# Encoder trunk on one Trainium2 core: the last expert's gate in two column halves, the last two blocks' norm steps shared, and a fixed order of ScalarE and VectorE at the end

## Chip, core and metric

The kernel runs on one core of a Trainium2 chip. The core has TensorE (PE; its weight loads are shown apart as PEld), VectorE (DVE), ScalarE (ACT), GpSimd (POOL) and SyncE (SP), and each works through its own queue in order. The metric is the device time of one execution in microseconds, less is better.

## The reference, cut to what matters

One layer of an encoder trunk over 512 tokens of 1024 numbers: a mixer, then 16 experts of which each takes the 64 tokens that like it best, then an embedding that is gated per token, and a last norm.

```python
def rmsnorm(x, g):
    y = xf * lax.rsqrt(jnp.mean(xf * xf, axis=-1, keepdims=True) + EPS)
    return (y * g.astype(jnp.float32)).astype(x.dtype)
...
        x = x + expert_choice_ffn(rmsnorm(x, norm2_g[i]), w_router[i], w_e_gate[i],
                                  w_e_up[i], w_e_down[i])
        gate = jax.nn.sigmoid(rmsnorm(x, norm3_g[i]) @ w_ple_gate[i])
        x = x + gate * (p[i] @ w_ple_proj[i])
    return rmsnorm(x, final_g)
```

The change lies in the last three lines. The sigmoid is made of a tanh: sigmoid(v) = 0.5 (1 + tanh(v / 2)).

## The kernel before, in words

The tokens stand in four blocks of 128 rows, `X[0]` to `X[3]`, each 128 x 1024. Experts 0 to 13 are added into the blocks in pairs. The rows of the last two experts, 14 and 15, go another way: the 64 tokens of each are gathered into a tile `xg[0]` or `xg[1]` of 128 x 512 (a token's 1024 columns lie in two partitions, 64 apart), the expert's output is added there, gate and last norm are done on that tile, and the rows are scattered into the output by GpSimd. So at the end two streams of work run beside each other: the four blocks, and the two tiles of rows.

For the blocks `base(i, k0, k1)` multiplies with the gate's weight (`w_ple_gate`, split into high and low parts by `gsplit`, three products for each): i = 0, 1 are the two column halves of blocks 0 and 1, i = 2, 3 those of blocks 2 and 3. Its sums stand in two PSUM tiles `zb[i][0]` and `zb[i][1]`, one for each block, and after the last product ScalarE copies them to SBUF, into `Z` (L1135; the profile names those tiles `w`). The loop at the end then does for each block b and half h: tanh (L1541, scaled with `r3`, half of the reciprocal root of the mean square), times the projected embedding plus one (L1542, VectorE), the addition to `X` (L1543, VectorE), and a square with a sum (`sumsq`, L983, ScalarE; its second record is the read of the accumulator). From the two sums of a block `rstd` makes the last norm's factor by three Newton steps, some ten short VectorE instructions that follow one another (L254 to L269), and VectorE multiplies the block by factor and weight at once (L1550). Blocks 0 and 1 are stored by SyncE, blocks 2 and 3 by GpSimd with an indirect DMA (`store`, L1521), since rows that the last experts took must be left out.

For the tiles of rows, `finish_start` transposes, `finish_gate` multiplies (`paired`, L1247: 16 products of 512 columns, with 64-wide weights, two records for each), `finish_gated` does tanh (L1412), times the embedding (L1413), addition (L1414) in two halves of 256 columns, sums of squares, and the product with the weight (L1416); `row_rstd` adds the sums across the partitions on TensorE (L1382) and makes the root, and `finish_end` scales (L1421). Row tile 14 is finished while `base(3, ...)` runs; `c15`, the gate of expert 15, is TensorE's last large product.

What sets the order: a scheduler places the instructions of each engine by the order in which the program is written, and by priority where data are ready; `later(n)` puts what is inside n places back. TensorE alone has an order by hand: `in_order` chains all of its instructions after `mark` as they are written.

Of the kernel before, what the change touches and what calls it, by code (L numbers as in the profile page):

```python
# [12 lines left out]
AF = mybir.ActivationFunctionType  # L13
ALU = mybir.AluOpType
# [35 lines left out]
TAIL = (4, 5, 6, 7) + (8,) + (9, 10, 11, 12, 13, 4, 5, 6) + (7, 9, 10, 11) + (12,)  # L50
SOON = 3
FAR = 4096.0
SM = {}


# [137 lines left out]
def in_order(tc, nc, mark, engine):  # L193

    last, on = None, False
    for i in list(nc.cur_bb.bb.instructions):
        if on and i.engine == engine:
            if last is not None:
                tc.add_manual_dep(i, last.name, mybir.DependencyInfo(
                    mybir.DependencyClass.NoSync, mybir.DependencyReason.DATA), reason="in order")  # L200
            last = i
        on = on or i is mark
# [7 lines left out]
def _body(ctx, tc, nc, A, out):  # L210
# [7 lines left out]
    def ps(tag):  # L218
        return psum.tile([128, 512], F32, name=f"ps_{tag}", tag=tag, bufs=NBANK[tag])
# [24 lines left out]
    def small(n, tag, dt=F32, bufs=8):  # L244
        return tiny.tile([128, 16], dt, name=tag, tag=tag, bufs=bufs)[:, :n]
# [331 lines left out]
    @contextmanager  # L577
    def later(n):
        c = tc.cur_priority
        tc.cur_priority = c + n  # L580
        yield
        if n:
            tc.cur_priority = c
# [398 lines left out]
    def sumsq(t, acc, junk):  # L982
        act.activation(junk, t, AF.Square, accum_out=acc)  # L983
# [136 lines left out]
    def base(i, k0, k1):  # L1120
        bp, h = divmod(i, 2)
        if k0 == 0:
            zb[i] = [ps("b"), ps("b")]
            if h == 0:
                z = place()
                Z.extend([z[:, 0:1024], z[:, 1024:2048]])
        for k in range(k0, k1):
            gh, gl = (ahead.pop(0) if ahead else gsplit(k, h))[:2]
            for j in range(2):
                hi, lo = xps[2 * bp + j, k // 4]  # L1130
                t = slice((k % 4) * 128, (k % 4 + 1) * 128)
                mm3(zb[i][j], hi[:, t], lo[:, t], gh, gl, k == 0, k == 7)
        if k1 == 8:
            for j in range(2):
                act.copy(Z[2 * bp + j][:, h * 512:(h + 1) * 512], zb[i][j])  # L1135

# [262 lines left out]
    def finish_factor(a):  # L1399

        r = row_rstd(a, "u")
        dve.tensor_scalar(r, r, 0.5, None, op0=ALU.mult)  # L1402
        return r

    def finish_gate(c, xgT, k0, k1):
        paired(c, xgT.rearrange("p (a b c) -> p a b c", a=4, b=2), [halves(w) for w in WG], k0, k1,
               (0, 4, 1, 5, 2, 6, 3, 7))

    def finish_gated(i, x_, c, r, zg, junk):

        for s in (slice(0, 256), slice(256, 512)):
            act.activation(zg[:, s], c[:, s], AF.Tanh, scale=r)  # L1412
            dve.scalar_tensor_tensor(zg[:, s], zg[:, s], 1.0, ppg[i][:, s], op0=ALU.add, op1=ALU.mult)  # L1413
            dve.tensor_add(x_[:, s], x_[:, s], zg[:, s])  # L1414
        a = row_sums(x_, "w", junk)
        dve.tensor_mul(x_, x_, fin)  # L1416
        return a

    def finish_end(x_, a):

        dve.tensor_scalar(x_, x_, row_rstd(a, "w"), None, op0=ALU.mult)  # L1421
# [81 lines left out]
    finish_gate(c14, xgT, 0, 8)  # L1503
    a15 = finish_start(xg[1], xgT2, zg2)
    a14 = finish_gated(0, xg[0], c14, r14, y14, xgT)
    base(3, 0, 4)
    r15 = finish_factor(a15)
    finish_end(xg[0], a14)
    base(3, 4, 8)
    c15 = ps("mm")  # L1510
    finish_gate(c15, xgT2, 0, 8)
    finish_end(xg[1], finish_gated(1, xg[1], c15, r15, zg2, xgT2))

    in_order(tc, nc, mark, pe.engine)


    stores = []

# [5 lines left out]
            tc.declare_no_dep(i.ins, j.ins, reason="the stores' rows are disjoint")  # L1524
        stores.append(i)

    s3 = small(8, "s3", bufs=1)
    for b in range(4):
        for h in range(2):
            s = slice(h * 512, (h + 1) * 512)  # L1530
            sumsq(X[b][:, s], s3[:, b * 2 + h:b * 2 + h + 1], nat)
    s3b = small(4, "s3b", bufs=1)
    dve.reduce_sum(s3b, s3.rearrange("p (b h) -> p b h", h=2), axis=AX.X)
    r3 = small(4, "r3", bufs=1)
    dve.tensor_scalar(r3, rstd(s3b, 1.0 / D), 0.5, None, op0=ALU.mult)
    for b in range(4):
        s4 = small(2, "s4", bufs=2)
        for h in range(2):
            s = slice(h * 512, (h + 1) * 512)
            z = Z[b][:, s]  # L1540
            act.activation(z, z, AF.Tanh, scale=r3[:, b:b + 1])  # L1541
            dve.scalar_tensor_tensor(z, z, 1.0, pp[b][h], op0=ALU.add, op1=ALU.mult)  # L1542
            dve.tensor_add(X[b][:, s], X[b][:, s], z)  # L1543
            sumsq(X[b][:, s], s4[:, h:h + 1], nat)
        s4b = small(1, "s4b", bufs=2)
        dve.tensor_add(s4b, s4[:, 0:1], s4[:, 1:2])
        r4 = rstd(s4b, 1.0 / D)
        for h in range(2):
            s = slice(h * 512, (h + 1) * 512)
            dve.scalar_tensor_tensor(X[b][:, s], X[b][:, s], r4, gfb[h], op0=ALU.mult, op1=ALU.mult)  # L1550
        if b < 2:
            sp.dma_start(rows(out, b), X[b])
        else:
            store(out, xi[b - 2], X[b], T - 1)
    for i in range(2):
        store(out.rearrange("t (h d) -> (t h) d", h=2), dsti[i], xg[i], 2 * T - 1)

# [20 lines left out]
```

## Time and profile before

| what | us |
|---|---|
| median of 3 runs | 1073.98 |
| lowest and highest | 1073.71, 1075.87 |
| the profiled execution, its own time | 1077.42 |
| its span, first to last instruction | 1075.6 |
| TensorE busy | 1004.6 (93%) |
| VectorE busy | 485.4 (45%) |
| ScalarE busy | 336.5 (31%) |
| GpSimd busy | 38.4 (4%) |

All times in rows are microseconds from the span's start, and all are of the profiled execution. The runs without the profiler are some 3 us shorter. A row of a timeline gives start, busy time, engine, line and operation, what it writes and reads, the shape, and in brackets how long the engine had been idle and who ended that.

### The profile page before, as it was taken

Reading aid. Unit: us, or ns where it says so; the run is one execution under the profiler, and the core shown is the slowest. Engines: PE = TensorE matmul, PEld = TensorE weight load, DVE = VectorE, ACT = ScalarE, POOL = GpSimd, SP = SyncE. Lnnn points to the kernel's source line nnn. Section 1 sums busy time; section 2 is a strip of 40 time slices with the busy share of each in tenths; the row PEclk is TensorE's granted clock in tenths of the full one; section 3 lists DMA queues with packets and bytes.
Section 4 is the critical chain, followed back from the end, with each engine's and each line's share of the span. In section 5 each row is a group of like instructions: output and inputs, shape, how many; then the busy total and the mean of one; then the engine's idle time right before and its main releaser. Section 6 shows DMA issues by size and latency. Waiting matters only on the chain.

```text
span 1075.6 us, 12115 instructions
## 1 busy us (share of the span) xinstructions
PE 1004.6 (93%) x4566; PEld 601.4 (56%) x4566; DVE 485.4 (45%) x1082; ACT 336.5 (31%) x624; POOL 38.4 (4%) x45
## 2 busy tenths in 40 slices
PE   8999999999999999999499999998887898999996
PEld 5777887787668788878333333443232333346453
DVE  6896786645765545635710110221020204044646
ACT  6343325426553323423111112011101012145443
POOL 0022011000000000000000000000000000000001
PEclk9999999999999999999789999999999899999998
DMA  9322121322122653463879989999999999999601
GB/s 313 125 79 79 40 71 65 102 80 83 54 79 78 202 178 99 157 237 103 313 299 406 424 339 425 424 425 425 425 426 424 424 424 428 422 410 425 260 1 50
DMA packets 55491, 264.15 MB, mean 246 GB/s; under 512 B 6715, under 2 KB 11579, under 8 KB 31880
## 3 DMA queue, kind: packets, MB, share of 16 engines
q1 hardware_dynamic: 51072, 252.14, 59.1%
q0 software_dynamic: 1904, 6.44, 1.5%
q10 hardware_dynamic: 2456, 4.79, 1.4%
q8 instruction: 36, 0.59, 0.2%
q14 instruction: 23, 0.19, 0.0%
HBM read 258.88 MB, written 4.72 MB: 245 GB/s over the span
## 4 chain that ended last, share of the span: by engine, by line
PE 71%; DMA 17%; DVE 7%; ACT 2%; issue 2%; POOL 0%; POOLq 0%; SPq 0%; DVEq 0%; ACTq 0%
PE ps_mm L1230 12%; DMA w<-in_w_gu_dram 11%; PE ps_y L1247 8%; PE ps_mm L414 8%; PE ps_mm L413 8%; PE ps_mm L412 7%; DMA w<-in_w_dn_dram 4%; PE ps_b L412 3%; PE ps_b L413 3%; PE ps_b L414 3%; PE ps_pj L412 2%; PE ps_pj L413 1%; PE ps_mm L995 1%; PE ps_pj L414 1%; PE ps_mm L993 1%
## 5 line engine op out<-in xcount | busy, mean ns | idle before, releaser
L1230 PE MATMUL ps_mm<-w,xt 128*64 128x512 f32 x992 | 222.5, 596 | 17.1 <-DMA w<-in_w_gu_dram 17.1
L1230 PEld LDWEIGHTS ps_mm<-w,xt 128*64 128x64 f32 x992 | 70.7, 137 | 165.8 <-issue 124.0
L412 PE MATMUL ps_mm<-hhi,whi 128*128 128x512 f32 x392 | 156.9, 400 | 0.6 <-ACT whi L327 0.6
L414 PE MATMUL ps_mm<-hhi,wlo 128*128 128x512 f32 x392 | 155.3, 397 | 0.7 <-DVE wlo L329 0.5
L413 PE MATMUL ps_mm<-hlo,whi 128*128 128x512 f32 x392 | 154.7, 395 | 0.2 <-DVE hlo L363 0.2
L1234 DVE TENSOR_TENSOR sg<-sg,ps_mm 128x512 f32<-128x512 f32 x16 | 11.0, 688 | 262.3 <-PE ps_mm L1230 262.3
L1247 PE MATMUL ps_y<-w,hd 128*64 128x512 f32 x480 | 109.0, 607 | 6.2 <-ACT hd L1255 6.2
L327 ACT CAST whi<-w 128x1024 fp32r<-128x1024 f32 x50 | 52.6, 1051 | 123.6 <-PE ps_mm L413 64.7
L412 PEld LDWEIGHTS ps_mm<-hhi,whi 128*128 128x128 f32 x392 | 74.2, 189 | 19.6 <-ACT whi L327 2.1
L414 PEld LDWEIGHTS ps_mm<-hhi,wlo 128*128 128x128 f32 x392 | 74.0, 189 | 18.7 <-issue 2.5
L413 PEld LDWEIGHTS ps_mm<-hlo,whi 128*128 128x128 f32 x392 | 74.1, 189 | 17.8 <-issue 2.5
L1247 PEld LDWEIGHTS ps_y<-w,hd 128*64 128x64 f32 x480 | 34.9, 139 | 70.5 <-issue 61.5
L1233 ACT ACTIVATE sg<-ps_mm 128x512 f32<-128x512 f32 x16 | 9.6, 597 | 181.6 <-PE ps_mm L1230 181.6
L329 DVE TENSOR_TENSOR wlo<-w,whi 128x1024 fp32r<-128x1024 f32 x49 | 60.1, 1229 | 6.4 <-ACT whi L327 6.2
L1265 ACT ACTIVATE ys<-ps_y,ia 64x512 f32<-64x512 f32 x28 | 19.1, 682 | 100.2 <-PE ps_y L1247 99.8
L625 DVE TENSOR_TENSOR sg<-ps_mm,rbs 128x512 f32<-128x512 f32 x32 | 22.1, 689 | 47.3 <-PE ps_mm L414 46.8
L1094 DVE TENSOR_TENSOR yh<-ys,yh 128x512 fp32r<-128x512 f32 x14 | 9.1, 689 | 70.6 <-ACT yh L1093 70.0
L1115 DVE SCALAR_TENSOR_TENSOR gl<-w,sm,gh 128x512 fp32r<-128x512 f32 x32 | 24.0, 751 | 21.8 <-ACT gh L1114 21.7
L1166 POOL DMA_INDIRECT xe<-h2d,iai x8 | 7.7, 964 | 681.6 <-DVE num L1086 373.4
L1114 ACT ACTIVATE gh<-w,sm 128x512 fp32r<-128x512 f32 x32 | 23.0, 723 | 28.0 <-PE ps_b L414 20.4
L626 ACT ACTIVATE sg<-sg,hbg 128x512 f32<-128x512 f32 x32 | 23.1, 721 | 12.8 <-DVE sg L625 12.8
L413 PE MATMUL ps_b<-gl,xTh 128*128 128x512 f32 x64 | 26.3, 410 | 0.2 <-DVE uo L1402 0.2
(505 smaller groups left out, 1522.5 us busy)
## 6 DMA issues: line engine op xcount, KB each, us to landing
w<-in_w_gu_dram SPq DMA_DIRECT2D x124, 1024.0 KB, 19.6
w<-in_w_dn_dram SPq DMA_DIRECT2D x60, 1024.0 KB, 19.6
w<-in_w_in_dram SPq DMA_DIRECT2D x50, 512.0 KB, 4.1
wb<-in_w_br_dram SPq DMA_DIRECT2D x32, 128.0 KB, 2.4
w<-in_w_out_dram SPq DMA_DIRECT2D x8, 512.0 KB, 4.1
we<-in_w_dn_dram SPq DMA_DIRECT2D x16, 256.0 KB, 8.4
we<-in_w_gu_dram SPq DMA_DIRECT2D x16, 256.0 KB, 6.1
w<-in_w_ple_gate_dram SPq DMA_DIRECT2D x4, 1024.0 KB, 21.1
```

The lines of the kernel that those rows point to most:

```text
L327: act.copy(hi, raw)
L329: (pool if key in PW else dve).tensor_sub(lo, raw, hi.bitcast(F32))
L412: pe.matmul(p, whi, mhi, start=start, stop=False)
L413: pe.matmul(p, whi, mlo, start=False, stop=False)
L414: pe.matmul(p, wlo, mhi, start=False, stop=stop)
L625: dve.tensor_mul(g, p, rbs)
L626: act.activation(g, g, AF.Tanh, bias=hbg[:, n * 8 + d:n * 8 + d + 1], scale=0.5)
L1114: i = act.activation(hi, v, AF.Copy, scale=S("g3", k))
L1115: dve.scalar_tensor_tensor(lo, v, S("g3", k), hi.bitcast(F32), op0=ALU.mult, op1=ALU.subtract)
L1230: pe.matmul(t[h * 64:(h + 1) * 64], x, w[k][h], start=k == 0, stop=k == 7)
L1247: pe.matmul(y[h * 64:(h + 1) * 64], lt[:, k % 4, k // 4, :], w[k][h], start=n == 0, stop=n == 7)
L1265: act.activation(ys[h][r], y[hs], AF.Copy, scale=ia[hs, 16 + e:17 + e])
```

## The change

The gate of expert 15 is written as two sets of products, for the columns 0 to 255 and 256 to 511 of the same PSUM tile `c15`. The first column halves of blocks 2 and 3 are carried further at once, up to the square and the product with the weight. For their second halves the copy out of PSUM goes: the tanh reads `zb[3]` itself. For blocks 2 and 3 the weight is multiplied before the root is known (`weighed`), both blocks' roots are made together in instructions of two columns, and the factor is applied last: one half of block 2 on VectorE, the other half and block 3 on ScalarE. What follows the gate is written in one order by hand, and `in_order` now holds ScalarE and VectorE to it from `mark2` on. The blocks' steps before that stand earlier in the text, inside `later(FL)`.

```diff
--- before.py
+++ after.py
@@ -50,6 +50,7 @@
 TAIL = (4, 5, 6, 7) + (8,) + (9, 10, 11, 12, 13, 4, 5, 6) + (7, 9, 10, 11) + (12,)
 SOON = 3
 FAR = 4096.0
+FL = 400
 SM = {}
 
 
@@ -1130,7 +1131,7 @@
                 hi, lo = xps[2 * bp + j, k // 4]
                 t = slice((k % 4) * 128, (k % 4 + 1) * 128)
                 mm3(zb[i][j], hi[:, t], lo[:, t], gh, gl, k == 0, k == 7)
-        if k1 == 8:
+        if k1 == 8 and i < 3:
             for j in range(2):
                 act.copy(Z[2 * bp + j][:, h * 512:(h + 1) * 512], zb[i][j])
 
@@ -1503,16 +1504,6 @@
     finish_gate(c14, xgT, 0, 8)
     a15 = finish_start(xg[1], xgT2, zg2)
     a14 = finish_gated(0, xg[0], c14, r14, y14, xgT)
-    base(3, 0, 4)
-    r15 = finish_factor(a15)
-    finish_end(xg[0], a14)
-    base(3, 4, 8)
-    c15 = ps("mm")
-    finish_gate(c15, xgT2, 0, 8)
-    finish_end(xg[1], finish_gated(1, xg[1], c15, r15, zg2, xgT2))
-
-    in_order(tc, nc, mark, pe.engine)
-
 
     stores = []
 
@@ -1524,34 +1515,98 @@
             tc.declare_no_dep(i.ins, j.ins, reason="the stores' rows are disjoint")
         stores.append(i)
 
-    s3 = small(8, "s3", bufs=1)
-    for b in range(4):
-        for h in range(2):
-            s = slice(h * 512, (h + 1) * 512)
-            sumsq(X[b][:, s], s3[:, b * 2 + h:b * 2 + h + 1], nat)
-    s3b = small(4, "s3b", bufs=1)
-    dve.reduce_sum(s3b, s3.rearrange("p (b h) -> p b h", h=2), axis=AX.X)
-    r3 = small(4, "r3", bufs=1)
-    dve.tensor_scalar(r3, rstd(s3b, 1.0 / D), 0.5, None, op0=ALU.mult)
-    for b in range(4):
-        s4 = small(2, "s4", bufs=2)
-        for h in range(2):
-            s = slice(h * 512, (h + 1) * 512)
-            z = Z[b][:, s]
-            act.activation(z, z, AF.Tanh, scale=r3[:, b:b + 1])
-            dve.scalar_tensor_tensor(z, z, 1.0, pp[b][h], op0=ALU.add, op1=ALU.mult)
-            dve.tensor_add(X[b][:, s], X[b][:, s], z)
-            sumsq(X[b][:, s], s4[:, h:h + 1], nat)
-        s4b = small(1, "s4b", bufs=2)
-        dve.tensor_add(s4b, s4[:, 0:1], s4[:, 1:2])
-        r4 = rstd(s4b, 1.0 / D)
-        for h in range(2):
-            s = slice(h * 512, (h + 1) * 512)
-            dve.scalar_tensor_tensor(X[b][:, s], X[b][:, s], r4, gfb[h], op0=ALU.mult, op1=ALU.mult)
-        if b < 2:
+    def embedded(b, h, g):
+
+        s = slice(h * 512, (h + 1) * 512)
+        z = Z[b][:, s]
+        act.activation(z, g, AF.Tanh, scale=r3[:, b:b + 1])
+        dve.scalar_tensor_tensor(z, z, 1.0, pp[b][h], op0=ALU.add, op1=ALU.mult)
+        dve.tensor_add(X[b][:, s], X[b][:, s], z)
+
+    def squares(b, h):
+        sumsq(X[b][:, h * 512:(h + 1) * 512], s4[:, b * 2 + h:b * 2 + h + 1], nat)
+
+    def weighed(b, h):
+        s = slice(h * 512, (h + 1) * 512)
+        dve.tensor_mul(Z[b][:, s], X[b][:, s], gfb[h])
+
+    s4 = small(8, "s4", bufs=1)
+    s4b = small(4, "s4b", bufs=1)
+    with later(FL):
+        s3 = small(8, "s3", bufs=1)
+        for b in range(4):
+            for h in range(2):
+                s = slice(h * 512, (h + 1) * 512)
+                sumsq(X[b][:, s], s3[:, b * 2 + h:b * 2 + h + 1], nat)
+        s3b = small(4, "s3b", bufs=1)
+        dve.reduce_sum(s3b, s3.rearrange("p (b h) -> p b h", h=2), axis=AX.X)
+        r3 = small(4, "r3", bufs=1)
+        dve.tensor_scalar(r3, rstd(s3b, 1.0 / D), 0.5, None, op0=ALU.mult)
+        for b in range(2):
+            for h in range(2):
+                embedded(b, h, Z[b][:, h * 512:(h + 1) * 512])
+                squares(b, h)
+            dve.tensor_add(s4b[:, b:b + 1], s4[:, 2 * b:2 * b + 1], s4[:, 2 * b + 1:2 * b + 2])
+            r4 = rstd(s4b[:, b:b + 1], 1.0 / D)
+            for h in range(2):
+                s = slice(h * 512, (h + 1) * 512)
+                dve.scalar_tensor_tensor(X[b][:, s], X[b][:, s], r4, gfb[h], op0=ALU.mult, op1=ALU.mult)
             sp.dma_start(rows(out, b), X[b])
-        else:
-            store(out, xi[b - 2], X[b], T - 1)
+        for b in range(2, 4):
+            embedded(b, 0, Z[b][:, 0:512])
+            squares(b, 0)
+            weighed(b, 0)
+    base(3, 0, 4)
+    r15 = finish_factor(a15)
+    finish_end(xg[0], a14)
+    base(3, 4, 8)
+
+    c15 = ps("mm")
+    halved = [slice(0, 256), slice(256, 512)]
+    WH = [halves(w) for w in WG]
+    xt15 = xgT2.rearrange("p (a b c) -> p a b c", a=4, b=2)
+    a15 = small(2, "wa", bufs=2)
+    mark2 = nc.cur_bb.bb.instructions[-1]
+
+    def gate15(s):
+        paired(c15[:, s], xt15, [[w[:, s] for w in ws] for ws in WH], order=(0, 4, 1, 5, 2, 6, 3, 7))
+
+    def tanh15(s):
+        act.activation(zg2[:, s], c15[:, s], AF.Tanh, scale=r15)
+
+    def add15(s):
+        dve.scalar_tensor_tensor(zg2[:, s], zg2[:, s], 1.0, ppg[1][:, s], op0=ALU.add, op1=ALU.mult)
+        dve.tensor_add(xg[1][:, s], xg[1][:, s], zg2[:, s])
+
+    gate15(halved[0])
+    gate15(halved[1])
+    embedded(2, 1, zb[3][0])
+    embedded(3, 1, zb[3][1])
+    squares(2, 1)
+    tanh15(halved[0])
+    weighed(2, 1)
+    squares(3, 1)
+    add15(halved[0])
+    sumsq(xg[1][:, halved[0]], a15[:, 0:1], xgT2[:, halved[0]])
+    dve.tensor_add(s4b[:, 2:4], s4[:, 4:8].rearrange("p (b h) -> p b h", h=2)[:, :, 0],
+                   s4[:, 4:8].rearrange("p (b h) -> p b h", h=2)[:, :, 1])
+    weighed(3, 1)
+    r4 = rstd(s4b[:, 2:4], 1.0 / D)
+    tanh15(halved[1])
+    dve.tensor_scalar(Z[2][:, 0:512], Z[2][:, 0:512], r4[:, 0:1], None, op0=ALU.mult)
+    act.activation(Z[2][:, 512:1024], Z[2][:, 512:1024], AF.Copy, scale=r4[:, 0:1])
+    add15(halved[1])
+    sumsq(xg[1][:, halved[1]], a15[:, 1:2], xgT2[:, halved[1]])
+    dve.tensor_mul(xg[1], xg[1], fin)
+    for h in range(2):
+        s = slice(h * 512, (h + 1) * 512)
+        act.activation(Z[3][:, s], Z[3][:, s], AF.Copy, scale=r4[:, 1:2])
+    finish_end(xg[1], a15)
+    in_order(tc, nc, mark, pe.engine)
+    for engine in (act.engine, dve.engine):
+        in_order(tc, nc, mark2, engine)
+    for b in range(2):
+        store(out, xi[b], Z[2 + b], T - 1)
     for i in range(2):
         store(out.rearrange("t (h d) -> (t h) d", h=2), dsti[i], xg[i], 2 * T - 1)
 
```

ScalarE at the end, before, from the copy of block 3's last sums on (`X_3267` and `X_3268` are blocks 2 and 3, `w_6904` their `Z`; what an instruction waits for is in brackets):

```order
L1135 COPY w_6904<-ps_b 128x512 [waits PE_49]
L1541 ACTIVATE w_6904<-w_6904,r_7196 128x512 [waits Activation_49]
L983 ACTIVATE nat,s_7270<-X_3267 128x512 [waits DVE_49]
L983 ACTIVATE nat,s_7300<-X_3268 128x512 [waits Activation_49]
L983 ACTIVATE nat,s_7300<-X_3268 128x512 [waits DVE_49,Activation_49]
L1412 ACTIVATE zg<-ps_mm,uo 128x256 [waits PE_49]
L1412 ACTIVATE zg<-ps_mm,uo 128x256
L983 ACTIVATE xgT,wa<-xg 128x256 [waits DVE_49] x2
```

And in the changed kernel (L1522 is the blocks' tanh, L1575 the gate's, L1597 and L1603 the scales):

```order
L1522 ACTIVATE w_6904<-ps_b,r_7049 128x512 [waits PE_49] x2
L984 ACTIVATE nat,s_7036<-X_3267 128x512 [waits DVE_49]
L1575 ACTIVATE zg<-ps_mm,uo 128x256 [waits PE_49]
L984 ACTIVATE nat,s_7036<-X_3268 128x512 [waits DVE_49,Activation_49]
L984 ACTIVATE xgT,wa<-xg 128x256 [waits DVE_49]
L1575 ACTIVATE zg<-ps_mm,uo 128x256
L1597 ACTIVATE w_6904<-w_6904,ro 128x512 [waits DVE_49]
L984 ACTIVATE xgT,wa<-xg 128x256 [waits DVE_49]
L1603 ACTIVATE w_6904<-w_6904,ro 128x512 x2
```

The square of block 3's second half stood ahead of the gate's first tanh and stands behind it now; the second tanh of the gate has no wait of its own in either.

VectorE at the end, before, from the end of block 3's root on:

```order
L269 SCALAR_TENSOR_TENSOR ro<-rt,ri 128x1 [waits DVE_49]
L1550 SCALAR_TENSOR_TENSOR X_3268<-X_3268,ro,gfb 128x512 [waits DVE_49]
L1413 SCALAR_TENSOR_TENSOR zg<-zg,ppg 128x256 [waits Activation_49] x2
L1414 TENSOR_TENSOR xg<-xg,zg 128x256 [waits DVE_49] x2
L1550 SCALAR_TENSOR_TENSOR X_3268<-X_3268,ro,gfb 128x512
L1416 TENSOR_TENSOR xg<-xg,fin 128x512 [waits Activation_49]
L254 TENSOR_SCALAR wv<-ps_t 128x1 [waits PE_49]
```

And in the changed kernel, first up to the start of the shared root (L1531 is `weighed`, L1578 and L1579 are `add15`, L1591 adds both blocks' sums):

```order
L1531 TENSOR_TENSOR w_6904<-X_3267,gfb 128x512
L1578 SCALAR_TENSOR_TENSOR zg<-zg,ppg 128x256 [waits Activation_49]
L1579 TENSOR_TENSOR xg<-xg,zg 128x256 [waits DVE_49]
L1591 TENSOR_TENSOR s4b<-s_7036 128x2 [waits Activation_49]
L1531 TENSOR_TENSOR w_6904<-X_3268,gfb 128x512
L255 TENSOR_SCALAR rv<-s4b 128x2 [waits DVE_49]
```

and then from its last step on:

```order
L270 SCALAR_TENSOR_TENSOR ro<-rt,ri 128x2 [waits DVE_49]
L1596 TENSOR_SCALAR w_6904<-w_6904,ro 128x512 [waits DVE_49]
L1578 SCALAR_TENSOR_TENSOR zg<-zg,ppg 128x256 [waits Activation_49]
L1579 TENSOR_TENSOR xg<-xg,zg 128x256 [waits DVE_49]
L1600 TENSOR_TENSOR xg<-xg,fin 128x512 [waits Activation_49]
L255 TENSOR_SCALAR wv<-ps_t 128x1 [waits PE_49]
```

Both halves of the gate's multiply and addition stood together, behind the two roots; now the first half stands ahead of the shared root (twelve instructions) and the second behind it.

## Rows read from the trace of the kernel before

**Rows 1.** The page, its fourth part: the chain that ended last, by engine.
```profile
PE 71%; DMA 17%; DVE 7%; ACT 2%; issue 2%; POOL 0%; POOLq 0%; SPq 0%; DVEq 0%; ACTq 0%
```

**Rows 2.** By stage: length; busy PE, PEld, DVE, ACT, POOL; granted clock, DMA share, GB/s.
```profile
1057.25:1064.35 7.10, 7.09 (x33) 2.21 (x32) 6.08 (x24) 4.09 (x9) 0.00 (x0) 1.00 0.08 32
...
1069.00:1075.60 6.60, 0.00 (x0) 0.00 (x0) 1.85 (x10) 0.00 (x0) 1.60 (x2) 0.51 0.26 104
```

**Rows 3.** Timeline of GpSimd, the last three stores.
```profile
1064.61 1.03 POOL L1521 DMA_INDIRECT out_dram<-X,numi  x1 [7.86 <-DVE ri L269]
1068.36 1.25 POOL L1521 DMA_INDIRECT out_dram<-X,numi  x1 [2.72 <-DVE X L1550]
1071.41 0.99 POOL L1521 DMA_INDIRECT out_dram<-xg,numi  x1 [1.80 <-DVE xg L1421]
```

**Rows 4.** Timeline of TensorE: the gate of expert 15, and the sums of squares.
```profile
1057.25 7.09 PE L1247 MATMUL ps_mm<-w,xgT 128*64 128x512 f32 x32
1067.68 0.78 PE L1382 MATMUL ps_t<-wa,one 128*128 128x1 f32 x4 [3.35 <-ACT xgT L983]
```

**Rows 5.** Timeline of ScalarE from 1044 us on.
```profile
1044.00 0.47 ACT L1412 ACTIVATE xe<-ps_pj,uo 128x256 f32<-128x256 f32 x1 [10.93 <-PE ps_pj L1247]
...
1056.65 0.59 ACT L1135 COPY w<-ps_b 128x512 f32<-128x512 f32 x1 [1.62 <-PE ps_b L414]
1057.27 0.72 ACT L1541 ACTIVATE w<-w,r 128x512 f32<-128x512 f32 x1
...
1060.99 0.63 ACT L983 ACTIVATE nat<-X 128x512 f32<-128x512 f32 x1
1061.53 0.19 ACT L983 ACTIVATION_READ_ACCUMULATOR nat<-X 128x1 f32 x1
1064.38 0.84 ACT L1412 ACTIVATE zg<-ps_mm,uo 128x256 f32<-128x256 f32 x2 [2.67 <-PE ps_mm L1247]
...
1067.54 0.40 ACT L983 ACTIVATE xgT<-xg 128x256 f32<-128x256 f32 x1
1067.84 0.19 ACT L983 ACTIVATION_READ_ACCUMULATOR xgT<-xg 128x1 f32 x1
```

**Rows 6.** Timeline of VectorE from 1056 us on.
```profile
1058.03 0.69 DVE L1542 SCALAR_TENSOR_TENSOR w<-w,grow 128x512 f32<-128x512 f32 x1 [2.21 <-ACT w L1541]
1058.76 0.69 DVE L1543 TENSOR_TENSOR X<-X,w 128x512 f32<-128x512 f32 x1
1059.36 0.69 DVE L1542 SCALAR_TENSOR_TENSOR w<-w,pp 128x512 f32<-128x512 f32 x1
1060.08 0.69 DVE L1543 TENSOR_TENSOR X<-X,w 128x512 f32<-128x512 f32 x1
...
1065.33 0.75 DVE L1550 SCALAR_TENSOR_TENSOR X<-X,ro,gfb 128x512 f32<-128x512 f32 x1
1066.00 0.75 DVE L1413 SCALAR_TENSOR_TENSOR zg<-zg,ppg 128x256 f32<-128x256 f32 x2
...
1068.67 0.15 DVE L254 TENSOR_SCALAR wv<-ps_t 128x1 f32<-128x1 f32 x1
...
1070.64 0.49 DVE L1421 TENSOR_SCALAR xg<-xg,wo 128x512 f32<-128x512 f32 x1
```

**Rows 7.** Timeline of VectorE, its idle time under TensorE's products near 1035 us.
```profile
1037.13 0.88 DVE L1501 SCALAR_TENSOR_TENSOR xg<-ps_y,ia,xg 128x256 f32<-128x256 f32 x2 [2.94 <-PE ps_y L1247]
```

**Rows 8.** Timeline of TensorE: short products with 64-wide weights.
```profile
171.26 0.44 PE L719 MATMUL ps_y<-PTn,vch 64*64 64x128 f32 x4
171.63 0.70 PE L691 MATMUL ps_b<-na 64*128 64x256 f32 x2
```

**Rows 9.** Chain of work that ended last, in order of time: eight transposes.
```profile
1001.26 1.09 PE ps_t L1100 x8
```

**Rows 10.** Timeline of VectorE: a root of four columns.
```profile
958.57 0.16 DVE L266 TENSOR_TENSOR rt<-ri 128x4 f32<-128x4 f32 x1
...
960.34 0.17 DVE L1535 TENSOR_SCALAR r<-ro 128x4 f32<-128x4 f32 x1
```

## The prediction, as it was made

> **What bounds the kernel now.** The page first: TensorE carries 71% of the chain that ended last [rows 1]. The reader should see that the change touches none of this except the last product; so the next view is the table by stage, which shows where TensorE stops: in 1057.25 to 1064.35 it is busy 7.09 of 7.10 us, from 1069.00 on not at all [rows 2]. Only the 11.3 us between the gate's end and the end of the span (1075.6) and the idle time of ScalarE and VectorE beside the gate can move. GpSimd's timeline names the three last stores: starts at 1064.61, 1068.36 and 1071.41 [rows 3], each about 0.28 us after its data (the last: L1421 ends at 1070.64 + 0.49 = 1071.13 [rows 6]). From the start of the last store to the end of the span it is 4.19 us, which I keep. So the question is when the last store can start, and that is a chain: gate's end, tanh (1064.38), multiply and add, squares, sums on TensorE, reciprocal root, scale (1070.64) [rows 4 to 6]. In it VectorE is the late engine: the tanh's first half is out at 1064.85 (1064.38 + 0.47), yet the multiply starts at 1066.00, since VectorE was still on block 3's norm (L1550 at 1065.33) [rows 5, 6]. About 1.1 us of the tail is lost there; the change goes for this.
>
> **The change part by part.** The order of TensorE, SyncE and GpSimd is the same but for the split gate, and up to 1055 us ScalarE and VectorE differ in three instructions only.
>
> *First halves of blocks 2 and 3, early.* Two weight products (0.69 us each) and one square join VectorE and ScalarE at about 1033 us. VectorE sits idle there for 2.94 us until TensorE's product is out at 1037.13 [rows 7]; 2 x 0.69 = 1.38 us fits. Cost nothing; uncovered it would be 1.4 us.
>
> *Two copies out of PSUM go.* ScalarE's tanh reads PSUM directly: 0.62 us earlier per block (the tanh starts at 1057.27 behind a copy that started at 1056.65 [rows 5]). The blocks' last halves on VectorE, which took 1058.03 to 1060.77 [rows 6], then end near 1060.0, plus a weight product of 0.60: 1060.6. After that VectorE has nothing that is ready until a tanh of the gate. The gain is real and falls into idle time.
>
> *The gate in halves.* 32 records of 512 columns become 64 of 256. By columns alone the length stays at 7.09 us, 0.11 us each. Four products of 64 columns wide and 128 long, each with its weight load, go by in 0.37 us (they start at 171.26, what follows at 171.63), 0.09 each [rows 8]; eight transposes take 1.09 us, 0.136 each [rows 9]. So the bounds are 7.1 and 64 x 0.136 = 8.7 us, +0 to +1.6. I take 0: the nearer row is the one with the same 64-wide weights, and 0.09 is under 0.11.
>
> *The wait.* This is where it turns. The halves share one PSUM tile. In the built order the tanh of the first half (L1575) waits for TensorE, and the tanh of the second half waits for nobody, although it reads what TensorE writes last: so the first one's wait already covers the whole gate. TensorE indeed raises its semaphore once, at the last product of the second half. The first tanh therefore starts at the same 1064.38 as before, not 3.5 us earlier.
>
> What the trace shows of such reads: ScalarE's read of the gate starts at 1064.38, behind the end of all its records at 1057.25 + 7.09 = 1064.34 [rows 4, 5]; no row here has a reader in a bank that TensorE is writing. [...]
>
> *What is queued behind it.* ScalarE's order is now fixed: the tanh of half 0 stands ahead of the square of block 3's second half. Before, that square ran at 1060.99 to 1061.72 [rows 5], under the gate. Now it waits for the gate's end, and with it, on VectorE in its fixed order: the sum of squares, the weight product of block 3, the shared root, block 2's scale, and only then the multiply of the gate's half 1. So the cover of the norm work, the gate, is gone. Worked out from the tanh's start T = 1064.38:
> - tanh of 256 columns 0.47 (its like at 1044.00 [rows 5]), multiply 0.04 + 0.42, add starts at T + 0.97 (0.04 is the gap between dependent instructions, as 1058.03 + 0.69 to 1058.76 [rows 6]).
> - Sum of squares 0.34 behind the add, T + 1.31. Its square started at about T + 0.37 and needs 0.73 (1060.99 to the end of its accumulator read at 1061.72 [rows 5]), so it is there at T + 1.10.
> - Weight product at T + 1.38; the next instruction can start 0.60 later (1058.76 to 1059.36 [rows 6]): T + 1.98.
> - The shared root: 12 instructions one behind the other. With four columns nine of them take 958.57 to 960.34, 0.196 each [rows 10]; 12 x 0.196 = 2.35: T + 4.33. Before it was two roots of ten short ones each, mostly under the gate.
> - Block 2's scale on VectorE, some 0.42 until the next can start (its like, L1421, takes 0.49 [rows 6]): T + 4.75. Multiply 0.46, add 0.42: T + 5.63.
> - Squares of half 1: 0.03 + 0.50 as 1067.54 to 1068.03 [rows 5]: T + 6.16. From there to the root 0.64 (1068.03 to 1068.67) and from the root to the scale 1.97 (1068.67 to 1070.64) [rows 6]: T + 8.77.
>
> Before, the scale stood at 1070.64, T + 6.26. The sum is **+2.51 us**. It can also be read so: the gate's last multiply starts 3.13 us later (T + 4.75 against T + 1.62) and gets back 0.62 since only one half follows it instead of two.
>
> *Stores.* Block 2's store is released by ScalarE's scale (L1597) near T + 5.0, block 3's by two scales (L1603) of 0.7 us behind the last squares, near T + 7.5, so GpSimd at 1072.1 instead of 1068.36. The last store would start at 1071.41 + 2.51 = 1073.92, 1.8 us behind it. The record of such a store takes 0.99 to 1.25 us [rows 3], which fits; but the shortest distance that rows show is 3.05 us (1068.36 to 1071.41). Bounds: +0 (record length) to +1.3 (3.05 against 1.8); I take 0, because in both pairs the later store's data came 0.28 us ahead of its start, so GpSimd waited for data and not for itself.
>
> *The sums on TensorE.* They come after some 6 us of idling instead of 3.3. [...] Four such records take 0.78 us [rows 4], and half of them lie on the path: 0 to +0.4, I take 0.
>
> The profiled execution took 1077.42 us (span 1075.6) against a median of 1073.98; I carry the difference over: 1073.98 + 2.5 = **1076.5 us**, 0.23% more. About 0.2%, 2.15 us, is what a measurement of this kernel can tell from no change.
>
> **The rivals.**
> *The halves overlap after all*, that is, the first tanh starts when half 0 is done (the other side: not slower). Then T is 1057.25 + 3.55 + 0.05 = 1060.85, and by the same sum the last multiply may start at 1065.60 (the second tanh is out at 1064.85), the scale at 1065.60 + 4.02 = 1069.62, 1.02 us sooner: 1073.0 us. It turns where the first tanh starts before 1064.38 - 2.51 = 1061.87. For it speaks that the code asks for two halves; against it the missing wait on the second tanh. 0.06.
> *GpSimd becomes the late one*: it can't take the last store until 3.05 us after block 3's. Then the last store starts near 1075.2: +3.8, 1077.8 us. Against it the 0.28 us above. 0.10.
> *The short products cost*: 64 at 0.136 us: T moves by 1.6, +4.1, 1078.1 us. Against it the row of 64-wide weights. 0.10.
>
> **How the numbers follow.** The forecast has 0.74. Within it the sum is uncertain by some half a microsecond (a dozen gaps read off rows, the clock's 0.4), and the three runs of before lie between 1073.71 and 1075.87; with the threshold at 2.15, close under 2.51, I give 0.48 of its 0.74 to slower, 0.24 to within and 0.02 to faster. GpSimd and the short products add 0.18 to slower and 0.02 to within, the overlap 0.04 to within and 0.02 to faster: slower 0.66, same 0.30, faster 0.04. The range reaches from 1074.9, between the overlap and the forecast, up to 1078.1, the dearest rival.
>
> **What the profile after would show.** The first L1575 tanh starts within 0.1 us of the gate's end and not in its middle; the square of block 3 behind it; VectorE idle from about 1060.6 to 1064.9; twelve short instructions after the gate's end instead of mostly before; the last multiply some 4.7 us behind the first tanh; the stores of block 3 and of the rows 1.8 us apart. I am wrong if the tanh starts near 1061, if the gate takes much over 7.1 us, or if the last store starts later than 0.3 us behind its scale.

## The result, and the profile after

The changed kernel takes 1080.74 us (median; 1079.41 to 1082.22), the kernel before on the same chip 1074.25 (1073.71 to 1077.11): a ratio of 1.0053, with a 95% interval of 1.0038 to 1.0068. It is slower, as forecast, but by 6.5 us instead of 2.5, and the time lies above the range. The profiled execution took 1081.15 us (span 1079.4) against 1077.42 (span 1075.6) before.

The page of the changed kernel, span, busy time by engine and the chain that ended last by engine (answers to [rows 1]):

```profile
span 1079.4 us, 12174 instructions
PE 1002.0 (93%) x4598; PEld 601.4 (56%) x4598; DVE 485.0 (45%) x1074; ACT 337.1 (31%) x625; POOL 38.4 (4%) x45
PE 72%; DMA 18%; DVE 6%; ACT 3%; issue 1%; POOL 0%; POOLq 0%; SPq 0%; DVEq 0%; ACTq 0%
```

This part of the page hardly differs from before; it doesn't show where 6 us went. So the timelines of the last stretch come next. Each row: start, busy us, engine, line, operation, tiles, shapes, and in brackets the idle time ahead of it and what ended it. TensorE, changed kernel (before: [rows 4]):

```profile
1058.36 7.13 PE L1248 MATMUL ps_mm<-w,xgT 128*64 128x256 f32 x64
1067.52 0.38 PE L1383 MATMUL ps_t<-wa,one 128*128 128x1 f32 x2 [2.03 <-ACT xgT L984]
1071.75 0.59 PE L1383 MATMUL ps_t<-wa,one 128*128 128x1 f32 x2 [3.85 <-ACT xgT L984]
```

ScalarE, changed kernel (before: [rows 5]):

```profile
1065.53 0.47 ACT L1575 ACTIVATE zg<-ps_mm,uo 128x256 f32<-128x256 f32 x1 [4.86 <-PE ps_mm L1248]
1065.90 0.62 ACT L984 ACTIVATE nat<-X 128x512 f32<-128x512 f32 x1
...
1067.37 0.46 ACT L1575 ACTIVATE zg<-ps_mm,uo 128x256 f32<-128x256 f32 x1
```

VectorE, changed kernel (before: [rows 6]); L1578 is the gate's multiply, L1531 block 3's weight product, L255 to L270 the shared root, L1422 the last scale:

```profile
1066.04 0.42 DVE L1578 SCALAR_TENSOR_TENSOR zg<-zg,ppg 128x256 f32<-128x256 f32 x1 [4.20 <-ACT zg L1575]
...
1066.91 0.68 DVE L1531 TENSOR_TENSOR w<-X,gfb 128x512 f32<-128x512 f32 x1
1067.51 0.16 DVE L255 TENSOR_SCALAR rv<-s4b 128x2 f32<-128x2 f32 x1
...
1069.87 0.49 DVE L1596 TENSOR_SCALAR w<-w,ro 128x512 f32<-128x512 f32 x1
1070.28 0.42 DVE L1578 SCALAR_TENSOR_TENSOR zg<-zg,ppg 128x256 f32<-128x256 f32 x1
...
1074.35 0.48 DVE L1422 TENSOR_SCALAR xg<-xg,wo 128x512 f32<-128x512 f32 x1
```

GpSimd's three last stores, changed kernel (before: [rows 3]):

```profile
1071.16 1.02 POOL L1512 DMA_INDIRECT out_dram<-w,numi  x1 [13.28 <-DVE xg L1579]
1073.19 0.98 POOL L1512 DMA_INDIRECT out_dram<-w,numi  x1 [1.01 <-ACT w L1603]
1075.11 0.99 POOL L1512 DMA_INDIRECT out_dram<-xg,numi  x1 [0.94 <-DVE xg L1422]
```

The tail is as forecast. The first tanh starts 0.04 us behind the gate's end (1058.36 + 7.13 = 1065.49), not in its middle; the square of block 3 stands behind it; the first multiply and the second are 4.24 us apart, with the root between them. From the gate's first product to the last scale it is 15.99 us instead of 13.39 (1070.64 - 1057.25), to the end of the span 21.04 instead of 18.35: **+2.7 us behind the gate's start.**

The rest must lie ahead of it. I took two marks that both kernels have on TensorE: the first record of the first of the products `ps_b<-yh,sel` near 722 us, and the start of the 48 records of `ps_mm<-w,xt` near 957 us. Before:

```profile
722.52 0.50 PE L1272 MATMUL ps_b<-yh,sel 128*128 128x512 f32 x1
956.16 10.52 PE L1230 MATMUL ps_mm<-w,xt 128*64 128x512 f32 x48
```

After:

```profile
720.59 0.50 PE L1273 MATMUL ps_b<-yh,sel 128*128 128x512 f32 x1
957.28 10.52 PE L1231 MATMUL ps_mm<-w,xt 128*64 128x512 f32 x48
```

The changed kernel is 1.93 us ahead at the first mark and 1.12 us behind at the second, and so it stays up to the gate (1058.36 against 1057.25). It lost 3.05 us between the marks, where not one instruction is changed. How early a kernel passes the first mark scatters from execution to execution: two_banks below has the same instructions up to there as the changed kernel and passes it at 723.69 us, 3.10 later. The table by stage between the marks (length; busy PE, PEld, DVE, ACT, POOL; granted clock, DMA share, GB/s), before:

```profile
722.52:956.16 233.64, 204.41 (x906) 78.64 (x905) 45.70 (x83) 40.37 (x73) 4.62 (x7) 0.98 1.01 425
```

after:

```profile
720.59:957.28 236.69, 204.40 (x907) 77.76 (x905) 45.69 (x83) 40.34 (x73) 4.63 (x7) 0.99 1.01 420
```

The engines do the same work in the same time, and TensorE's mean granted clock is no lower after (0.99 of full speed) than before (0.98), so the clock did not cost the 3 us. The DMA share is 1.01 in both, all 16 DMA engines without a pause, but they move 420 GB/s instead of 425. What TensorE waits for is in the page's costliest groups (busy, mean ns, idle time ahead and its releaser), before:

```profile
L1230 PE MATMUL ps_mm<-w,xt 128*64 128x512 f32 x992 | 222.5, 596 | 17.1 <-DMA w<-in_w_gu_dram 17.1
```

after:

```profile
L1231 PE MATMUL ps_mm<-w,xt 128*64 128x512 f32 x992 | 222.9, 596 | 20.2 <-DMA w<-in_w_gu_dram 20.2
```

3.1 us more of waiting for the same weights. Here the experts' weights stream through a ring of 1 MB loads, 8 KB to each partition, and this stage ends when they have landed. The packet records of the trace say how long one 8 KB packet occupies its DMA engine: before, 78% of the 23552 take 309 ns or less, after 29%; the mean is 315.8 against 318.1 ns, and of those that start between the two marks 310.7 against 314.4 ns. On the stage's 233.64 us that makes 2.8 of the 3.05 us (an estimate: 233.64 x 3.7 / 310.7).

**What moved.** The diff replaces two small tags (`s4`, `s4b`) with two buffers each by tags with one: two tiles of 64 bytes per partition go. In the built programs everything that lies behind them on the left side of SBUF is therefore 128 bytes lower. Of the 14 places that weights are loaded into, the seven of the tags `w` and `w3` now start at 128 bytes past a multiple of 256 instead of at one; the seven of `w2` and `w4`, on the right side, stay at 32 past. Order and number of loads are the same. The theory to test: the forecast tail, +2.5 us, plus the shift, +3 to 4 us. The rival: the tail, the new order and the split gate cost all of it, and the loads' rate is chance.

### The profile page after: what moved, and what is told of

Read it like the earlier page. It is cut to its first block, busy times and chain, and to the rows that moved or that the text cites. A ratio compares the mean times of both kernels' runs of the same rounds, so it can differ in the third digit from the quotient of the medians.

```text
span 1079.4 us, 12174 instructions
## 1 busy us (share of the span) xinstructions
PE 1002.0 (93%) x4598; PEld 601.4 (56%) x4598; DVE 485.0 (45%) x1074; ACT 337.1 (31%) x625; POOL 38.4 (4%) x45
## 4 chain that ended last, share of the span: by engine, by line
PE 72%; DMA 18%; DVE 6%; ACT 3%; issue 1%; POOL 0%; POOLq 0%; SPq 0%; DVEq 0%; ACTq 0%
PE ps_mm L1231 12%; DMA w<-in_w_gu_dram 12%; PE ps_y L1248 8%; PE ps_mm L415 8%; PE ps_mm L414 7%; PE ps_mm L413 7%; DMA w<-in_w_dn_dram 4%; PE ps_b L413 3%; PE ps_b L414 3%; PE ps_b L415 3%; PE ps_pj L413 2%; PE ps_pj L414 1%; PE ps_mm L996 1%; PE ps_pj L415 1%; PE ps_mm L994 1%; PE ps_mm L995 1%
```

## The experiments

Ratios are to the kernel before on the same chip, with 95% intervals. "Last scale" and "end" are us behind the first product of expert 15's gate, worked out from each run's timelines; "stage" is the length between the two marks, one profiled execution each.

| run | median us (runs) | ratio | last scale | end | stage | packets at 309 ns or less |
|---|---|---|---|---|---|---|
| before | 1074.25 (5) | 1 | 13.39 | 18.4 | 233.64 | 78% |
| after | 1080.74 (5) | 1.0053 [1.0038, 1.0068] | 15.99 | 21.0 | 236.69 | 29% |
| again | 1081.66 (6) | 1.0064 [1.0048, 1.0081] | 16.00 | 21.0 | 235.37 | 30% |
| two_banks | 1078.54 (7) | 1.0037 [1.0022, 1.0052] | 12.51 | 17.5 | 236.32 | 28% |
| norm_first | 1077.62 (12) | 1.0025 [1.0013, 1.0036] | 12.74 | 17.8 | 236.39 | 29% |
| free_order | 1079.16 (6) | 1.0046 [1.0028, 1.0064] | 13.49 | 18.5 | 235.83 | 29% |
| before_shift | 1079.13 (12) | 1.0035 [1.0021, 1.0049] | 13.38 | 18.4 | 236.59 | 27% |
| after_pad | 1077.85 (12) | 1.0029 [1.0012, 1.0045] | 16.00 | 21.0 | 233.51 | 78% |
| banks_pad | 1075.02 (12) | 1.0002 [0.9988, 1.0016] | 12.51 | 17.5 | 233.36 | 78% |
| before_align | 1072.81 (12) | 0.9982 [0.9965, 0.9998] | 13.39 | 18.4 | 230.96 | 97% |
| banks_align | 1071.89 (6) | 0.9966 [0.9954, 0.9978] | 12.52 | 17.5 | 231.27 | 97% |
| root_under | 1069.87 (6) | 0.9955 [0.9937, 0.9973] | 11.73 | 16.7 | 231.36 | 97% |
| right64 | 1077.18 (1) | | 13.40 | 18.4 | 232.95 | 83% |

The stage alone sorts the kernels by where the weights land, whatever their tail: 235.37 to 236.69 us (420 GB/s in all six) with the seven places of `w` and `w3` at 128 past a multiple of 256, 233.36 to 233.64 (425) with those seven at one and the others at 32 past, 230.96 to 231.36 (426 to 427) with all 14 at one.

### The tail: again, two_banks, norm_first, free_order

**again** is the changed kernel once more, as the mark for the three others.

> The changed kernel once more, unchanged, beside the kernel before on the same chip. Theory A (the tail alone): the tail is longer by 2.6 us, counted from the start of expert 15's gate to the start of the last scale (15.99 us after, 13.39 before), and that is all the change does; the other 3 us of the measured 5.7 to 6.5 came from the chip or the moment (the weights' stage ran at 420 instead of 425 GB/s), so here the difference is 2.6 us, 0.24%. Theory B (something ahead of the gate is slowed by the change, its code or where its tiles and instructions lie): again 5.7 us, 0.53%.

1.0064: the loss is there again in new runs, no smaller than at first. Of theory A's two halves the 2.6 us of tail are there (16.00 against 13.39), the rest did not go away.

**two_banks** gives each half of the gate a PSUM tile of its own, and keeps the order.

```diff
-    c15 = ps("mm")
+    c15 = ps("mm"), ps("mm")
...
-        paired(c15[:, s], xt15, ...)
+        paired(c15[s.start // 256][:, s], xt15, ...)
...
-        act.activation(zg2[:, s], c15[:, s], AF.Tanh, scale=r15)
+        act.activation(zg2[:, s], c15[s.start // 256][:, s], AF.Tanh, scale=r15)
```

> The two column halves of expert 15's gate go into two PSUM banks instead of one; nothing else is changed. Theory A: the first tanh starts after half of the gate, 3.6 us after its first product instead of 7.2, and by the same steps the last scale stands at 3.64 + 4.75 + 4.02 = 12.4 us after the gate's first product, 3.6 sooner than in the changed kernel and 1.0 sooner than before: 1.0 us faster than before in all. If the shared bank is not what holds the tanh (rival: the matrix engine's queue or the hand-written order does), the tanh stays at 7.2 us and the time at that of the changed kernel. Theory B: 1.0 us of gain and 3 us of loss ahead of the gate, 2 us slower than before.

Timelines of two_banks, TensorE, ScalarE and VectorE:

```profile
1061.10 7.13 PE L1248 MATMUL ps_mm<-w,xgT 128*64 128x256 f32 x64
...
1064.82 0.47 ACT L1575 ACTIVATE zg<-ps_mm,uo 128x256 f32<-128x256 f32 x1 [1.42 <-PE ps_mm L1248]
...
1068.28 0.47 ACT L1575 ACTIVATE zg<-ps_mm,uo 128x256 f32<-128x256 f32 x1 [1.22 <-PE ps_mm L1248]
...
1069.57 0.42 DVE L1578 SCALAR_TENSOR_TENSOR zg<-zg,ppg 128x256 f32<-128x256 f32 x1
...
1073.61 0.49 DVE L1422 TENSOR_SCALAR xg<-xg,wo 128x512 f32<-128x512 f32 x1
```

The first tanh starts 3.72 us behind the gate's first product instead of 7.17, under the second half, and the last scale comes 3.48 us sooner than in the changed kernel and 0.88 sooner than before. So the shared tile had turned the halves into one. (The kernel counts such tiles as banks, in `NBANK`; whether the built order goes by tile or by bank is not told apart.) Yet the kernel is slower than before by 0.37%, although its tail is shorter: the tail is not the whole loss.

**norm_first** keeps one tile and puts the norm of blocks 2 and 3 (second square, shared root, block 2's scales) ahead of the gate's tanhs in the order written by hand.

```diff
     squares(2, 1)
-    tanh15(halved[0])
     weighed(2, 1)
     squares(3, 1)
-    add15(halved[0])
-    sumsq(xg[1][:, halved[0]], a15[:, 0:1], xgT2[:, halved[0]])
...
     r4 = rstd(s4b[:, 2:4], 1.0 / D)
-    tanh15(halved[1])
...
+    tanh15(halved[0])
+    add15(halved[0])
+    tanh15(halved[1])
+    sumsq(xg[1][:, halved[0]], a15[:, 0:1], xgT2[:, halved[0]])
     add15(halved[1])
```

> One bank as in the changed kernel, but in the order written by hand block 3's square, the shared root and block 2's scales stand ahead of the gate's two tanhs, so that they run under the gate. Theory A: the first tanh 7.2 to 7.4 us after the gate's first product (behind a scale on the scalar engine), the last scale 4.64 + 0.5 behind it, at 12.5 us: 3.5 us sooner than in the changed kernel, 0.9 us faster than before. Rival: the root itself (twelve instructions of two columns) is what costs; then the last scale stays near 16 us. Theory B: 3 us more in all, 2 us slower than before.

Timelines of norm_first, TensorE and VectorE:

```profile
1058.71 7.13 PE L1248 MATMUL ps_mm<-w,xgT 128*64 128x256 f32 x64
...
1063.12 0.16 DVE L255 TENSOR_SCALAR rv<-s4b 128x2 f32<-128x2 f32 x1
...
1065.49 0.48 DVE L1592 TENSOR_SCALAR w<-w,ro 128x512 f32<-128x512 f32 x1
...
1066.60 0.43 DVE L1578 SCALAR_TENSOR_TENSOR zg<-zg,ppg 128x256 f32<-128x256 f32 x1 [0.63 <-ACT zg L1575]
1067.41 0.42 DVE L1578 SCALAR_TENSOR_TENSOR zg<-zg,ppg 128x256 f32<-128x256 f32 x1
...
1071.45 0.48 DVE L1422 TENSOR_SCALAR xg<-xg,wo 128x512 f32<-128x512 f32 x1
```

The root begins at 1063.12, under the gate (which ends at 1065.84), and is over at about its end: the cover that, by the prediction, the changed kernel had lost is back, and the last scale comes at 12.74, 3.25 us sooner than with the tanh in front. Again the kernel stays slower than before, 0.25%.

**free_order** drops the fixed order on ScalarE and VectorE.

```diff
     in_order(tc, nc, mark, pe.engine)
-    for engine in (act.engine, dve.engine):
-        in_order(tc, nc, mark2, engine)
```

> The changed kernel without the hand-written order on the scalar and vector engines: the scheduler places them. It puts block 3's square, the root and all scales of blocks 2 and 3 ahead of the gate's tanhs. Theory A: the square runs under the gate again, but three scales of some 0.65 us stand ahead of the first tanh, which starts near 8.3 us after the gate's first product; the last scale near 13.5 us, 2.5 us sooner than in the changed kernel and as before: same time as before within 0.5 us. If the hand-written order does not matter, the last scale stays at 16 us. Theory B: 3 us slower than before.

Left to itself the built order does the norm first too, and its last scale stands at 13.49, within 0.1 us of before. With a tail equal to before's this kernel is still 0.46% slower. That is the cleanest sight of the second loss: 4.9 us (3.0 to 6.9 by the interval) that no instruction of the tail carries.

### The shift: before_shift, after_pad, banks_pad

The three differ from their parents by one line, which reserves small tiles that nobody uses, 128 bytes per partition, so that what lies behind them moves up. Each engine's instructions and their order stay as they were.

```diff
     def small(n, tag, dt=F32, bufs=8):
         return tiny.tile([128, 16], dt, name=tag, tag=tag, bufs=bufs)[:, :n]
 
+    small(1, "pad", bufs=2)
+
```

**before_shift** is the kernel before with it: now `w` and `w3` lie 128 bytes past a multiple of 256.

> The kernel before with one unused small tile of 2 x 64 bytes per partition in the pool of small tiles, nothing else: every engine's instructions and their order are the same, and all tiles that lie behind that pool on its side of SBUF, among them 7 of the 14 places for weight tiles, lie 128 bytes higher (their addresses modulo 256 are 128 instead of 0). Theory C (addresses): the changed kernel needs two tags of the small pool less, so these places lie 128 bytes lower there, also at 128 modulo 256; its weight packets of 8 KB take 313 to 315 ns where they took 309, 468 to 470 us of packets on each DMA engine against 465. Then this kernel shows the same: 420 GB/s on the plateau instead of 425, and 3 to 4 us more time than before, with its tail unchanged. Rival D (the changed kernel's instructions, their number or where they lie, slow the loads): no difference from the kernel before.

**after_pad** is the changed kernel with it: there `w` and `w3` come back to their places of before.

> The changed kernel with the same unused tile of 128 bytes, so that the weight tiles lie where they lay before; its instructions and their order are those of the changed kernel. Theory C: the plateau is back at 425 GB/s, packets at 309 ns, and what is left is the tail: 2.6 us more than before, some 4 us less than the changed kernel. Rival D: 6.7 us more than before, as the changed kernel.

The stage between the marks, before_shift:

```profile
722.46:959.05 236.59, 204.53 (x906) 77.95 (x904) 45.62 (x83) 40.33 (x73) 4.63 (x7) 0.99 1.01 420
```

after_pad:

```profile
721.48:954.99 233.51, 203.49 (x906) 78.30 (x904) 45.61 (x83) 40.33 (x73) 4.63 (x7) 0.99 1.01 425
```

An unused 128 bytes takes the kernel before from 425 to 420 GB/s and from 233.64 to 236.59 us in this stage, 0.35% in the whole; the same 128 bytes give the changed kernel 425 GB/s and 233.51 us back. What is left of the changed kernel's loss, 0.29% [0.12, 0.45], is 3.1 us: the tail, for which the profile says 2.6 to the last scale and 2.7 to the end. Shift and tail together make 0.64%, against 0.53% and 0.64% measured for the whole. The loss is told apart.

**banks_pad** is two_banks with the same line.

> The changed kernel with the gate's halves in two PSUM banks and the 128 bytes put back. Theory C with the tail as measured in the run of two banks: that run was 4.0 us slower than before; less the 4 us of the loads it is at the time of the kernel before or up to 1 us faster. Rival D: 4 us slower.

1.0002: the 0.9 us that its tail is shorter than before's is not seen in the times; the interval, -1.3 to +1.7 us, holds it just so. Against two_banks the pad is worth 0.35% once more.

### All places at multiples of 256: before_align, banks_align, root_under, right64

The right side's `w2` and `w4` start at 32 past a multiple of 256 in both kernels. **before_align** is the kernel before with 32 unused bytes at the upper end, so that all 14 places start at a multiple of 256.

```diff
+    ctx.enter_context(tc.tile_pool(name="edge", bufs=1, side="right")).tile([128, 8], F32, name="edge")
     ctxB = ctxR.enter_context(ExitStack())
```

> The kernel before with an unused tile of 32 bytes per partition at the upper end of SBUF: the other 7 places for weight tiles lie 32 bytes lower, at 0 modulo 256 (they lie at 32 modulo 256 before), so that all 14 do; instructions and order are the same. Theory C in its strict form (packets to an address that is a multiple of 256 take 309 ns, others 314): the packets that still took 313 to 320 ns (a fifth) go to 309, and the time falls by 1 to 3 us. Rival: only the 7 lower places matter, or the address modulo 64: no difference.

The stage between the marks, before_align:

```profile
718.74:949.70 230.96, 202.43 (x906) 77.17 (x904) 45.51 (x83) 40.31 (x73) 4.63 (x7) 0.99 1.01 426
```

97% of the packets take 309 ns or less, the stage is 2.7 us shorter than before's, and the kernel 0.18% faster [0.02, 0.35], 1.9 us. Packets that start between the marks take 309.4 ns on average instead of 310.7, which makes about 1 us of the 2.7 (an estimate: 233.64 x 1.3 / 310.7). TensorE is also busy 2.0 us less there, at a mean granted clock of 0.99 instead of 0.98; how the rest of the gain comes about is not shown, only that the 32 bytes bring it.

**right64** moves the right side by 96 bytes instead of 32 (`[128, 24]` in the line above), to 192 past a multiple of 256.

> The kernel before with 96 instead of 32 unused bytes at the upper end of SBUF: 7 weight places lie at 192 modulo 256, that is at a multiple of 64 but not of 128, and the other 7 at multiples of 256. If a multiple of 64 is enough, 97% of the 8 KB packets take 309 ns or less, as with all at multiples of 256; if it takes 256 (or 128 at least), 78% as in the kernel before, where these places lie at 32 modulo 256.

A single execution: 83% of the packets, 232.95 us in the stage. That is near before (78%, 233.64) and far from before_align, so a multiple of 64 is not enough.

**banks_align** is banks_pad with the 32 bytes too.

> The changed kernel with the gate's halves in two PSUM banks, the 128 bytes put back below and the 32 bytes added above, so that all 14 places for weight tiles lie at multiples of 256. The two causes add if they are independent: the tail of two banks ends 0.88 us sooner after the gate's first product than the kernel before (17.50 against 18.38), and the addresses alone gave 1.9 us: 2.8 us faster than before. If the gain of one is taken back by the other (the sooner gate waits for the same thing), 1.9 us or less.

0.9966 [0.9954, 0.9978]: 3.7 us faster than before, 2.4 to 4.9 by the interval. The sum of the two gains, 2.8 us, lies in it, and 1.9 us does not.

**root_under** is banks_align with another order by hand: the norm of blocks 2 and 3 ahead of the first half's multiply, so that the root runs under the gate's second half.

```diff
     squares(2, 1)
-    tanh15(halved[0])
     weighed(2, 1)
     squares(3, 1)
-    add15(halved[0])
-    sumsq(xg[1][:, halved[0]], a15[:, 0:1], xgT2[:, halved[0]])
+    weighed(3, 1)
+    tanh15(halved[0])
...
-    weighed(3, 1)
     r4 = rstd(s4b[:, 2:4], 1.0 / D)
+    act.activation(Z[2][:, 512:1024], Z[2][:, 512:1024], AF.Copy, scale=r4[:, 0:1])
+    add15(halved[0])
     tanh15(halved[1])
```

> As the run before (two banks, all weight tiles at multiples of 256), and in the order written by hand block 3's square stands ahead of the gate's first tanh and the shared root ahead of the first half's multiply, block 2's scale behind it: the whole root lies under the gate's second half. In two banks the last multiply starts at 8.47 us after the gate's first product, though its tanh is out at 7.68, since the vector engine is on the root and the scale until then. If that is what holds it, it starts at 7.7 now, the last scale at 11.7 instead of 12.5, and the kernel is 0.8 us faster than the run before, 3.6 us faster than before. If the root under the gate delays the first half instead, nothing is gained.

Timelines of root_under, TensorE, ScalarE and VectorE:

```profile
1050.92 7.13 PE L1251 MATMUL ps_mm<-w,xgT 128*64 128x256 f32 x64
...
1054.64 0.47 ACT L1578 ACTIVATE zg<-ps_mm,uo 128x256 f32<-128x256 f32 x1
...
1058.11 0.46 ACT L1578 ACTIVATE zg<-ps_mm,uo 128x256 f32<-128x256 f32 x1
...
1055.11 0.17 DVE L257 TENSOR_SCALAR rv<-s4b 128x2 f32<-128x2 f32 x1
...
1058.60 0.43 DVE L1581 SCALAR_TENSOR_TENSOR zg<-zg,ppg 128x256 f32<-128x256 f32 x1
...
1062.65 0.48 DVE L1425 TENSOR_SCALAR xg<-xg,wo 128x512 f32<-128x512 f32 x1
```

The second tanh starts at once when the gate ends (1058.05), its multiply 0.49 us behind it, and the last scale stands at 11.73, 1.66 us sooner than before's. With the places aligned this is the fastest of all: 1069.87 us, 0.9955 [0.9937, 0.9973], 4.8 us faster than before; the 3.6 expected lie within the interval. banks_align had 0.9966; the two intervals overlap, so the gain of the order alone, 0.8 us by the profile, is not shown by the times.

## Why the prediction was right in sign and wrong in size

**Right, term by term.** With T the start of the first tanh (1065.53):

| step | forecast | measured |
|---|---|---|
| T behind the gate's first product | 7.13 | 7.17 |
| block 3's weight product | T + 1.38 | T + 1.38 |
| the shared root starts | T + 1.98 | T + 1.98 |
| it is out, block 2's scale | T + 4.33 | T + 4.34 |
| second multiply | T + 4.75 | T + 4.75 |
| last squares are out | T + 6.16 | T + 6.17 |
| last scale | T + 8.77 | T + 8.82 |

The wait of the first tanh for the whole gate held, and two_banks shows its cause: with two tiles the tanh starts 3.45 us sooner (3.72 us behind the gate's first product, with one tile 7.17). In no timeline of these runs does a tanh of the gate read a tile that TensorE is still writing, so what such a read would do is not shown.

The bounds fell at their near ends. The gate in halves took 7.13 us against 7.09, so 64 short products cost 0.04 and not 1.6. The two last stores start 1.92 us apart, the last one 0.28 us behind the end of its data (1074.35 + 0.48), so GpSimd was not the late one. The second pair of sums on TensorE took 0.59 us where half of the four before is 0.39, 0.2 of the 0.4 that the bound allowed. No run shows that 0.4, which the prediction puts down to the clock; what they show is the 0.59. The granted clock was 1.00 of full speed when the first pair took 0.38; it averages 0.87 over the 4.30 us from 1067.50 on, in which TensorE was busy for 0.44, and 0.50 from 1071.8 us on. The first halves of blocks 2 and 3 that moved to about 1033 us cost nothing: from the second mark to the gate's start the two profiles keep their distance (1.12 and 1.11 us).

**Wrong.** The step that failed is the first part's sentence that only the 11.3 us between the gate's end and the end of the span can move, with its ground that the order of TensorE, SyncE and GpSimd is the same. The order was the same; the addresses were not. The chain had 17% of DMA in it [rows 1], so a stage in which the loads set the pace was in plain sight, and the prediction had no term for what could change a load. Of the two small tags of the diff that went from `bufs=2` to `bufs=1` the prediction says nothing. They moved seven of 14 weight places by 128 bytes: +3.05 us in the stage between the marks, 0.35% [0.21, 0.49], 3.8 us, of the whole by before_shift. With that term the sum would have been 2.5 + 3.8 = 6.3 us against 6.5 measured. None of the rivals held it, and the range, made of the tail's uncertainties alone, could not.

One more thing is wrong ahead of the sum, though it leaves the sum as it is: that the runs without the profiler are some 3 us shorter. In the eleven other sets of several runs the profiled execution lies between 1.9 us below and 1.9 us above its median, so the 3 us were the scatter of one execution. The spans of the two profiles differ by 3.8 us and the medians by 6.5, so subtracting whole spans would have hidden most of the second loss; the difference within one stage showed it.

## What to carry to other kernels

Where a stage streams weights with every DMA engine busy (a DMA share of 1.01 here), tiles that are added, dropped or made smaller ahead of the weight ring are part of the change: look at the addresses of the rings before and after, and keep the places at multiples of 256 bytes, as 32 unused bytes did here for 1.9 us (0.2 to 3.8). Splitting the gate by columns let its reader start early only with a PSUM tile for each half (3.72 us behind the first product); in one tile the first reader waited for both (7.17), and the order fixed by hand then held up everything behind it, so work that needs nothing of the product belongs ahead of that reader. Compare two traces between marks that both kernels have, not by their spans.

## What the runs showed of the hardware that I had not expected

Between the marks an 8 KB packet of a weight load takes 309 ns when all 14 places in SBUF start at a multiple of 256 bytes: in before_align the means by place are 309 to 310 ns, and the stage moves 426 GB/s. In the changed kernel and in before_shift, with seven places at 128 past and seven at 32 past, they are 313 to 316 ns, at 420 GB/s. It is the destination that moved between these kernels. The seven places at 128 past took 313 to 314 ns in the changed kernel; why a packet takes longer there is not shown.

For places at 32 past the trace gives no single figure. In the kernel before, the three `w4` places took just under 310 ns and the four `w2` places, at the same 32 past, 312 to 315; in the changed kernel `w4` took about 315 too, though it had not moved. By order of issue the slow packets of the kernel before stand together: the three `w4` loads follow seven aligned ones and are fast, and only within the `w2` loads behind them does the time rise to 314 ns and more, until the aligned loads come again. In right64 it is the same, with `w4` and `w2` at 192 past. Several loads are on their way at once (in the kernel before a 1 MB load lands 19.6 us after its issue, the median, while 1 MB at 425 GB/s makes some 2.5 us, an estimate from the stage's rate), and a grouping by load may mix neighbours. What a place off a multiple of 256 costs by itself beside aligned ones stays open; what is shown is the sum over the ring, in three pairs of kernels that differ by the 128 bytes, and in before_align.
